# Paired half-height matmuls, two-chunk recurrence steps and early sums of squares in a fused two-block network

## The chip, the core and the metric

The kernel runs on one core of a Trainium2 chip. The metric is the device time of one execution in microseconds (us). Engines are named as the profile names them: PE (TensorE matmuls), PEld (its weight loads), DVE (VectorE), ACT (ScalarE), POOL (GpSimd) and SP (SyncE). Matmul results land in PSUM, which the kernel uses as eight banks, a0 to a3 and d0 to d3; a view of the profile shows them as `ps_a` and `ps_d`.

## What is computed

Two residual blocks over 512 tokens of width 1024, in float32, each with its own mixture of experts. Block 1 mixes a gated linear recurrence (HGRN2) with differential attention; block 2 mixes an RWKV-7 recurrence with a sparse attention, then a cross attention. What the change touches:

```python
# HGRN2, chunks of 64 tokens, 4 heads of 128
o = tril(q_rel k_rel^T) v + (q * exp(b)) S          # value products
S = exp(b_end) * S + k_end^T v                       # state update
o = rms_norm(o)
# differential attention, 4 heads, key width 64, four query blocks of 128
a = softmax(q1 k1^T / 8) - lam * softmax(q2 k2^T / 8)
o = rms_norm(a v)
# block 2, RWKV: two low-rank products (64 -> 512); sparse attention: 8 heads of width 64
w, a = tanh(xw) @ w2, xa @ a2
p = softmax(q_h k_h^T / 8 + mask);  o_h = p v_h      # causal, masked to selected keys
```

## The kernel before

The program is written as stages in Python order, and a scheduler fixes one static instruction order for each engine: it simulates a time line and takes the next instruction that is ready there. An engine then runs its list strictly in that order and waits at each entry for what that needs. Only instructions given to `keep_in_program_order` keep the written order among themselves.

Block 1's dense part is this. The normalised input (`hT`) is multiplied with the projection weights in `dense`, whose matmuls all carry the line of `mm` (L209): three passes over 128 x 512 tiles, `hT,wh`, `hT,wl` and a low part of `hT` with `wh`. Call these the dense matmuls. They need nothing of the attention, so the scheduler puts them between the steps of it. The attention (L542 to L569) takes 16 iterations, four heads with four query blocks of 128; iteration i has n = 128(i+1) keys. Each does two score matmuls with 64 rows (L550, banks a0 and a1), a causal mask added by a matmul (L551), a maximum on DVE (L552), exponentials on ACT (L555), the combination on DVE (L558 to L560), i+1 transposes (L564, bank a2) and a copy on ACT (L565); after a head come four value matmuls (L568). `aT` and `dv` are kept, and a norm over them (L572 to L588) makes `C`, the input of the first branch product.

The recurrence (L635 to L669) runs over 4 pairs of chunks in bank a3 alone: chunk scores (L643), a masking multiply (L645), transposes of the keys (L648), and for each chunk four state products with 64 rows (L658), four updates on DVE (L661) and, for each head, a 64-row value product (L666) and a 128-row state product (L667). `out_norm` then makes the input of the second branch product, which lies in `D`. Behind it stand the first branch products (`ps_d<-C,wh`) and the second (`ps_d<-D,wh`).

In block 2 the low-rank products (L1322, L1326) have 64 rows each, in the lower and the upper half; the sparse attention (L1671 to L1700) has the same shape as block 1's, with two heads e = 0, 1 for each of four p: scores L1679, mask L1682, maximum L1684, exponential L1687, scaling L1689, transposes L1692 and their copy L1693, value products L1698. Its scores take banks d0, d1 and a2 in turn, its transposes d2 and a3. Dense matmuls (`hT`, later the 96 with `r` and `k`) stand between its steps. After it comes the branch product `ps_d<-GG,wh`. The experts' stages, which stream weights, are not touched.

Of the kernel before, what the change touches and what calls it, by code (L numbers as in the profile page):

```python
# [177 lines left out]
class Net:  # L178
# [29 lines left out]
    def mm(self, *a, **k):  # L208
        self.pin(self.nc.tensor.matmul(*a, **k))  # L209

# [197 lines left out]
    def dense1(self, rings, late):  # L408
# [129 lines left out]

        for h in range(4):
            vh = dv[:, :, h * 128:(h + 1) * 128]  # L540
            aT = B.tile([128, 4, 512], F32, name="aT", bufs=2)
            for i in range(4):  # L542
# [19 lines left out]
                b = self.bank("a2")  # L562
# [3 lines left out]
            b = self.bank("a2")  # L566
# [6 lines left out]
        r = A.tile([128, 4, 8], F32, name="onr", bufs=2)  # L573
        b = self.bank("a", (128, 4, 8))
        for h in range(4):
            sq = k3([128, 512])
            nc.scalar.activation(sq.rearrange("p (j n) -> p j n", j=4), vv(h), AF.Square)
            self.tok_sums(b, sq, 2 * h, one2)
        nc.scalar.activation(r, b, AF.Sqrt, scale=1.0 / 128, bias=self.eps)
        nc.vector.reciprocal(r, r)  # L580
        for h in range(4):
            b = self.tok_spread(r, 2 * h, 1)
# [14 lines left out]
        self.banks("a3")  # L597
# [37 lines left out]
        S = B.tile([128, 4, 128], F32, name="hgS", bufs=2)  # L635
        nc.vector.memset(S, 0.0)
        for m in range(4):
            tok = slice(m * 128, (m + 1) * 128)
            b = self.bank("a", (128, 4, 64))
            for h in range(4):  # L640
                for p in range(2):
                    c = slice(m * 128 + p * 64, m * 128 + p * 64 + 64)
                    nc.tensor.matmul(b[p * 64:(p + 1) * 64, h, :], krel[:, h, c], qrel[:, h, c], start=True, stop=True)  # L643
            sc = k2([128, 4, 64])
            nc.vector.tensor_mul(sc, b, self.c("inc64")[:, None, :].broadcast_to([128, 4, 64]))  # L645
# [4 lines left out]
            nc.scalar.activation(ke, b, AF.Copy)  # L650
            for p in range(2):
                r = slice(p * 64, (p + 1) * 64)
                c = slice(m * 128 + p * 64, m * 128 + p * 64 + 64)
                So = S
                if 2 * m + p < 7:
                    bk = self.bank("a", (128, 4, 128))
                    for h in range(4):
                        nc.tensor.matmul(bk[:, h, :], ke[r, h, :], hv[r, m, h * 128:(h + 1) * 128], start=True, stop=True)  # L658
                    S = B.tile([128, 4, 128], F32, name="hgS", bufs=2)
                    for h in range(4):  # L660
# [1240 lines left out]
```

## Time and profile before

| | us |
|---|---|
| median of 3 runs (lowest to highest) | 2191.87 (2190.04 to 2196.93) |
| the profiled execution | 2193.93 |
| its span | 2192.2 |
| first attention score to first branch product, block 1 | 109.2 to 369.6 |
| first to second branch product, block 1 | 369.6 to 393.7 |
| end of RWKV's solve to sparse attention's branch product, block 2 | 1331.4 to 1467.5 |

The profile is of one execution; its time less its span, 1.7 us, lies outside the span. "Granted clock" is a share of TensorE's full 2.4 GHz; 0.50 is its lower level, 1.2 GHz. A float32 matmul of narrow tiles is shown as two records, and a record's printed length overlaps the next one's, so the time that one takes is read from start to start.

### The profile page before, as it was taken

The page shows a single profiled execution, that of the slowest core. Times are in us where ns is not written, and L with a number is a line of the kernel's source. Part 1 is how long each engine was busy: PE and PEld are TensorE (multiplying, and loading weights), DVE is VectorE, ACT ScalarE, POOL GpSimd, SP SyncE. Part 2 cuts the span into 40 slices and gives each one's busy share as a digit, 9 for nine tenths or more (in the row PEclk, how much of TensorE's full clock was granted, in tenths as well). Part 3 has the DMA queues.
Part 4 walks back from the last instruction along what each step waited for, and adds up shares of the span by engine and source line. Part 5 has one row for each costly group of instructions (what it writes and reads, how often), then busy time and mean ns, then how long its engine had stood idle before and what let it go on. Part 6 is the DMA issues. An engine that isn't in the chain of part 4 may idle for free. (4 is left out here: it accounts for less than half of the span.)

```text
span 2192.2 us, 29816 instructions
## 1 busy us (share of the span) xinstructions
PE 2116.7 (97%) x11946; PEld 1363.0 (62%) x11946; DVE 983.7 (45%) x2002; ACT 679.4 (31%) x1317; POOL 161.6 (7%) x138
## 2 busy tenths in 40 slices
PE   8999999999999999998989999999898999999996
PEld 6766778787544444445766775677778454444443
DVE  4674323563333332325388484445455232333334
ACT  5463333253111111114534333433443111111112
POOL 0420001200000000000252100001110000000000
PEclk9999899999999999998999999999999999999998
DMA  4211131377999999993222112112633899999994
GB/s 178 87 66 48 46 109 67 143 287 269 415 419 417 420 420 419 420 377 106 68 76 77 40 63 77 39 65 77 250 110 141 345 409 420 420 419 420 419 419 162
DMA packets 96318, 505.87 MB, mean 231 GB/s; under 512 B 21088, under 2 KB 26208, under 8 KB 44464
## 3 DMA queue, kind: packets, MB, share of 16 engines
q1 hardware_dynamic: 90992, 490.09, 56.3%
q10 hardware_dynamic: 4688, 11.66, 1.5%
q0 software_dynamic: 496, 2.17, 0.3%
q8 instruction: 96, 1.57, 0.3%
q14 instruction: 46, 0.38, 0.0%
HBM read 494.83 MB, written 8.91 MB: 230 GB/s over the span
## 5 line engine op out<-in xcount | busy, mean ns | idle before, releaser
L209 PE MATMUL ps_d<-wslot,xg 128*64 128x512 f32 x2048 | 446.4, 592 | 0.0
L209 PE MATMUL ps_d<-hT,wh 128*128 128x512 f32 x1056 | 348.0, 414 | 1.9 <-DVE hT L300 1.9
L209 PEld LDWEIGHTS ps_d<-wslot,xg 128*64 128x64 f32 x2048 | 148.3, 137 | 286.5 <-issue 276.5
L195 DVE TENSOR_TENSOR wl<-wslot,wh 128x512 fp32r<-128x512 f32 x236 | 168.6, 719 | 287.4 <-ACT wh L194 232.0
L194 ACT ACTIVATE wh<-wslot 128x512 fp32r<-128x512 f32 x260 | 163.2, 630 | 320.9 <-PE ps_d L209 255.8
L209 PEld LDWEIGHTS ps_d<-hT,wh 128*128 128x128 f32 x1056 | 199.7, 195 | 54.7 <-issue 9.3
L1010 DVE TENSOR_TENSOR s<-ps_d,s 128x512 f32<-128x512 f32 x32 | 22.1, 692 | 423.0 <-PE ps_d L209 423.0
L209 PE MATMUL ps_d<-hT,wl 128*128 128x512 f32 x528 | 210.3, 410 | 0.5 <-DVE wl L195 0.5
L209 PE MATMUL ps_a<-wslot,hidT 128*64 128x512 f32 (+1 forms) x832 | 178.3, 578 | 1.7 <-ACT hidT L1018 1.4
L209 PE MATMUL ps_d<-wh,hT 128*128 128x512 f32 x512 | 164.1, 397 | 3.0 <-DVE hT L300 1.4
L1048 DVE TENSOR_TENSOR acc<-acc,ps_a 128x512 f32<-128x512 f32 (+1 forms) x214 | 131.2, 664 | 54.9 <-PE ps_a L209 54.7
L209 PEld LDWEIGHTS ps_a<-wslot,hidT 128*64 128x64 f32 x832 | 58.7, 137 | 108.9 <-issue 100.4
L209 PE MATMUL ps_a<-yy,S 128*128 128x512 f32 (+1 forms) x428 | 114.6, 400 | 5.6 <-DVE acc L1048 5.6
L209 PEld LDWEIGHTS ps_d<-hT,wl 128*128 128x128 f32 x528 | 102.7, 195 | 25.4 <-issue 1.9
L209 PEld LDWEIGHTS ps_d<-wh,hT 128*128 128x128 f32 x512 | 95.7, 188 | 26.7 <-ACT wh L194 1.7
L985 ACT ACTIVATE xg<-ps_a,gain 128x256 f32<-128x256 f32 x102 | 48.2, 475 | 200.0 <-PE ps_a L209 200.0
L209 PE MATMUL ps_a<-oh,xs 128*128 128x256 f32 x816 | 107.1, 285 | 1.3 <-DVE oh L1137 1.3
L209 PEld LDWEIGHTS ps_a<-oh,xs 128*128 128x128 f32 x816 | 100.9, 191 | 9.6 <-issue 9.6
L1036 ACT ACTIVATE yy<-ps_a,gc 128x512 fp32r<-128x512 f32 (+1 forms) x52 | 34.9, 671 | 223.7 <-PE ps_a L209 192.2
L209 PE MATMUL ps_d<-wl,hT 128*128 128x512 f32 x256 | 101.8, 397 | 1.8 <-DVE wl L195 1.8
L209 PEld LDWEIGHTS ps_a<-yy,S 128*128 128x128 f32 x428 | 74.8, 188 | 31.4 <-DVE acc L1048 13.6
L1009 ACT ACTIVATE s<-ps_d 128x512 f32<-128x512 f32 x32 | 19.1, 598 | 199.3 <-PE ps_d L209 199.3
(584 smaller groups left out, 2838.2 us busy)
## 6 DMA issues: line engine op xcount, KB each, us to landing
wslot<-in_wm_dram SPq DMA_DIRECT2D x380, 1024.0 KB, 11.6
wslot<-in_wd_dram SPq DMA_DIRECT2D x108, 512.0 KB, 3.6
wslot<-in_wd_dram SPq DMA_DIRECT2D x19, 1024.0 KB, 14.7
wslot<-in_wm_dram SPq DMA_DIRECT2D x8, 512.0 KB, 15.0
C<-in_x_dram SPq DMA_DIRECT2D x4, 512.0 KB, 5.2
acc<-in_x_dram ACTq DMA_DIRECT2D x4, 512.0 KB, 4.8
kvd<-kvs ACTq DMA_DIRECT2D x8, 256.0 KB, 4.1
xd<-acc ACTq DMA_DIRECT2D x1, 2048.0 KB, 11.9
```

Of the source, the lines that this page charges most:

```text
L194: self.nc.scalar.activation(hi, src, AF.Copy)
L195: (lo_eng or self.nc.vector).tensor_sub(lo, src, hi.bitcast(F32))
L209: self.pin(self.nc.tensor.matmul(*a, **k))
L985: nc.scalar.activation(xg[:, k, :n], b[:, :n], AF.Copy, scale=gain[:, k:k + 1])
L1009: nc.scalar.activation(s1, hb[0], AF.Silu)
L1010: nc.vector.tensor_mul(s1, hb[1], s1)
L1036: nc.scalar.activation(y[0][:, c], b, AF.Copy, scale=gcol)
L1048: nc.vector.tensor_add(acc[:, t, c], acc[:, t, c], b)
```

## The change

`side_by_side` issues two matmuls that use opposite row halves one after the other, upper half first, and keeps all such pairs in program order. It is used for the scores of both attentions, for the state products of two chunks, and for the low-rank products. In the attentions the transposes go into the bank of the scores; block 1's attention and recurrence now share all four a banks; the sparse attention takes (d0, d1) and (d2, a2) by turns. The recurrence treats two chunks as one step: the masked scores sit in a 128 x 128 block-diagonal tile (zeroed once on POOL), so that one full-height value product serves both chunks, and the state products add to the same bank. Squares and their sums are taken as each head or each pair of chunks ends.

```diff
+    def side_by_side(self, xs, stop=True):
+
+
+        for o, l, r in xs[::-1]:
+            self.tc.keep_in_program_order(self.nc.tensor.matmul(o, l, r, start=True, stop=stop))
...
+        def scales(r):
+
+            nc.scalar.activation(r, r, AF.Sqrt, scale=1.0 / 128, bias=self.eps)
+            nc.vector.reciprocal(r, r)
...
-                ps = []
-                for m in range(2):
-                    r = slice(m * 64, (m + 1) * 64)
-                    b = self.bank("a%d" % m)
-                    nc.tensor.matmul(b[:, :n], qkT[r, 0, h, qs], qkT[r, 1, h, :n], start=True, stop=False)
+                ps, sb = [], [self.bank("a") for _ in range(2)]
+                self.side_by_side([(sb[m][:, :n], qkT[m * 64:m * 64 + 64, 0, h, qs], qkT[m * 64:m * 64 + 64, 1, h, :n])
+                                   for m in range(2)], stop=False)
+                for m, b in enumerate(sb):
                     nc.tensor.matmul(b[:, qs], idb, dgn, start=False, stop=True)
                     nc.vector.reduce_max(st[:, m:m + 1], b[:, :n], axis=AX.X)
                     nc.vector.tensor_scalar(st[:, 2 + m:3 + m], st[:, m:m + 1], -0.125, None, op0=ALU.mult)
...
-                b = self.bank("a2")
+                b = sb[0]
...
-            b = self.bank("a2")
+            b = self.bank("a")
...
-        self.banks("a0", "a1", "a2")
+            sq = k4([128, 512])
+            nc.scalar.activation(sq, b, AF.Square)
+            b = self.bank("a", (128, 4, 2))
+            self.tok_sums(b, sq, 0, one2)
+            nc.vector.tensor_copy(rd[:, :, 2 * h:2 * h + 2], b)
...
+        scales(rd)
...
+        S = B.tile([128, 4, 128], F32, name="hgS", bufs=3)
...
+        scs = [k3([128, 4, 128]) for _ in range(2)]
+        for t in scs:
+            nc.gpsimd.memset(t, 0.0)
...
-            sc = k2([128, 4, 64])
-            nc.vector.tensor_mul(sc, b, self.c("inc64")[:, None, :].broadcast_to([128, 4, 64]))
+                    nc.tensor.matmul(b[rs[p], h, :], krel[:, h, cs[p]], qrel[:, h, cs[p]], start=True, stop=True)
+            sc = scs[m % 2]
+            for p in range(2):
+                nc.vector.tensor_mul(sc[rs[p], :, rs[p]], b[rs[p]],
+                                     self.c("inc64")[rs[p], None, :].broadcast_to([64, 4, 64]))
...
+
+            Ss = [S]
+            bks = [self.bank("a", (128, 4, 128)) for _ in range(2 if m < 3 else 1)]
+            for h in range(4):
+                hc = slice(h * 128, (h + 1) * 128)
+                self.side_by_side([(bk[:, h, :], ke[rs[p], h, :], hv[rs[p], m, hc]) for p, bk in enumerate(bks)])
+            for p, bk in enumerate(bks):
+                S = B.tile([128, 4, 128], F32, name="hgS", bufs=3)
+                for h in range(4):
+                    nc.vector.scalar_tensor_tensor(S[:, h, :], Ss[p][:, h, :], eend[:, h, 2 * m + p:2 * m + p + 1],
+                                                   bk[:, h, :], op0=ALU.mult, op1=ALU.add)
+                Ss.append(S)
+            bo = self.bank("a", (128, 4, 128))
+            for h in range(4):
+                nc.tensor.matmul(bo[:, h, :], hv[:, m, h * 128:(h + 1) * 128], sc[:, h, :], start=(h == 0), stop=False,
+                                 skip_group_check=True)
...
-                    for h in range(4):
-                        nc.tensor.matmul(bk[:, h, :], ke[r, h, :], hv[r, m, h * 128:(h + 1) * 128], start=True, stop=True)
-                    S = B.tile([128, 4, 128], F32, name="hgS", bufs=2)
-                    for h in range(4):
-                        nc.vector.scalar_tensor_tensor(S[:, h, :], So[:, h, :], eend[:, h, 2 * m + p:2 * m + p + 1],
-                                                       bk[:, h, :], op0=ALU.mult, op1=ALU.add)
-                bo = self.bank("a", (128, 4, 64))
                 for h in range(4):
-                    vh = hv[r, m, h * 128:(h + 1) * 128]
-                    nc.tensor.matmul(bo[:, h, :], vh, sc[r, h, :], start=True, stop=False)
-                    nc.tensor.matmul(bo[:, h, :], So[:, h, :], qe[:, h, c], start=False, stop=True)
-                nc.scalar.activation(oT[:, :, c], bo, AF.Copy)
+                    nc.tensor.matmul(bo[:, h, rs[p]], Ss[p][:, h, :], qe[:, h, cs[p]], start=False, stop=(p == 1 and h == 3),
+                                     skip_group_check=True)
+            nc.scalar.activation(oT[:, :, tok], bo, AF.Copy)
...
+            sq = k2([128, 4, 128])
+            nc.scalar.activation(sq, bo, AF.Square)
+            b = self.bank("a", (128, 8))
+            for h in range(4):
+                nc.tensor.matmul(b[:, 2 * h:2 * h + 2], sq[:, h, :], one2, start=True, stop=True)
+            nc.vector.tensor_copy(rh[:, m, :], b)
...
+        scales(rh)
...
-            b = self.bank("a")
-            nc.tensor.matmul(b, lora[0:64, pc], xw[0:64], start=True, stop=True)
+            wb = [self.bank("a") for _ in range(2)]
+            self.side_by_side([(wb[e], lora[e * 64:e * 64 + 64, pc], xw[e * 64:e * 64 + 64]) for e in range(2)])
...
+            bo_ = self.bank(("d3", "a3")[p % 2])
...
-                sb = []
-                for e in range(2):
-                    r = slice(e * 64, e * 64 + 64)
-                    b = self.bank(("d0", "d1", "a2")[(turn + e) % 3])
-                    nc.tensor.matmul(b[:, :n], qT[r, p, qs], KT[r, p, :n], start=True, stop=False)
-                    sb.append(b)
+                sb = [self.bank((("d0", "d1"), ("d2", "a2"))[turn % 2][e]) for e in range(2)]
+                turn += 1
+                self.side_by_side([(sb[e][:, :n], qT[e * 64:e * 64 + 64, p, qs], KT[e * 64:e * 64 + 64, p, :n])
+                                   for e in range(2)], stop=False)
...
-                    b = self.bank(("d2", "a3")[turn % 2])
```

The changed kernel's lines are some 6 to 11 higher than those of before; its pairs all carry L215. Two places show how the order moves on PE.

The first is in block 1. Before, on PE in the middle of the recurrence, attention scores and masks (L550, L551), dense matmuls (L209) and state products of a chunk (L658) stand among one another.

```order
L550 MATMUL ps_a_1091<-C 128x128
L551 LDWEIGHTS idb
L551 MATMUL ps_a_1091<-dgn,idb 128x128
L209 MATMUL ps_d_2030<-hT_92,wh 128x512
L209 MATMUL ps_d_2030<-hT_91,wl 128x512
L209 MATMUL ps_d_2031<-hT_91,wh 128x512
L658 MATMUL ps_a_1792<-F,k_1770 128x128
L550 MATMUL ps_a_1105<-C 128x256
L551 LDWEIGHTS idb
L551 MATMUL ps_a_1105<-dgn,idb 128x128
L658 MATMUL ps_a_1792<-F,k_1770 128x128 x3
```

Small and dense rows alternate here in groups of one to six.

After, at the end of block 1's attention (L215 on `C` scores, L561 mask, L574 transposes, L578 value products): the last dense matmul stands ahead of head 3's third set of transposes.

```order
L209 MATMUL ps_d_2591<-hT_92,wh 128x512
L209 MATMUL ps_d_2591<-hT_91,wl 128x512
L574 MATMUL ps_a_1138<-cst,k_1145 128x128 x3
L215 MATMUL ps_a_1161<-C 128x512
L215 MATMUL ps_a_1160<-C 128x512
L561 LDWEIGHTS idb
L561 MATMUL ps_a_1160<-dgn,idb 128x128
L561 LDWEIGHTS idb
L561 MATMUL ps_a_1161<-dgn,idb 128x128
L574 MATMUL ps_a_1160<-cst,k_1167 128x128 x4
L578 MATMUL ps_a_1182<-aT,dv 128x512
L578 MATMUL ps_a_1182<-aT,dv 128x384
```

Behind its first two rows no dense matmul follows until the first branch product: the scores of the last block stand behind the transposes of the one before.

Further on in the same list, the last two steps of the recurrence (L215 on `F` state products, L682 products with the state, L654 chunk scores, L661 key transposes, L689 sums, L678 value products) and the first branch product (`C,wh`):

```order
L215 MATMUL ps_a_1889<-F,k_1886 128x128
L215 MATMUL ps_a_1888<-F,k_1886 128x128
L682 MATMUL ps_a_1908<-E,hgS 128x64 x4
L654 MATMUL ps_a_1930<-acc 64x64 x8
L661 MATMUL ps_a_1941<-cst,D 128x128 x4
L689 MATMUL ps_a_1924<-one_680,k_1922 128x2 x4
L678 MATMUL ps_a_1958<-k_1747,F 128x128 x4
L215 MATMUL ps_a_1948<-F,k_1946 128x128 x4
L682 MATMUL ps_a_1958<-E,hgS 128x64 x8
L689 MATMUL ps_a_1974<-one_680,k_1972 128x2 x4
L209 MATMUL ps_d_2754<-C,wh 128x512 x2
L209 MATMUL ps_d_2754<-C,wl 128x512
```

So what stood among dense matmuls now stands behind them: 674 dense rows lie between the first score and the first branch product in both lists, in the changed one all of them ahead of the last two iterations' transposes and of the whole recurrence, in blocks of about 36 to 42 between two iterations.

Second place, the sparse attention on PE, before: one block's value products (L1698), another's transposes (L1692) and two others' scores (L1679) follow one another, with dense matmuls behind.

```order
L1698 MATMUL ps_d_10552<-GG_10275,X_8929 64x128 x7
L1692 MATMUL ps_a_10714<-cst,k_10710 128x128
L1679 MATMUL ps_a_10753<-VU,qT 128x384
L1692 MATMUL ps_d_10731<-cst,k_10727 128x128 x2
L1682 LDWEIGHTS X_7481
L1682 MATMUL ps_a_10753<-X_7481 128x384
L1679 MATMUL ps_d_10787<-VU,qT 128x512
L1682 LDWEIGHTS X_7481
L1682 MATMUL ps_d_10787<-X_7481 128x512
L209 MATMUL ps_a_11117<-r,wh 128x512
L209 MATMUL ps_a_11117<-k,wh 128x512
L209 MATMUL ps_a_11117<-r,wl 128x512
```

After, the same attention at p = 1 (L1698 transposes, L1703 value products, L215 scores, L1689 masks; `ps_a_10476` and `ps_d_10475` are the banks of the 512-key block):

```order
L1698 MATMUL ps_d_10441<-cst,k_10449 128x128 x3
L1698 MATMUL ps_d_10442<-cst,k_10461 128x128 x3
L1703 MATMUL ps_a_10384<-GG_10253,X_8907 64x128 x6
L215 MATMUL ps_a_10476<-VU,qT 128x512
L215 MATMUL ps_d_10475<-VU,qT 128x512
L1689 LDWEIGHTS X_7459
L1689 MATMUL ps_d_10475<-X_7459 128x512
L1689 LDWEIGHTS X_7459
L1689 MATMUL ps_a_10476<-X_7459 128x512
L1698 MATMUL ps_d_10475<-cst,k_10483 128x128 x4
L1698 MATMUL ps_a_10476<-cst,k_10496 128x128 x4
L1703 MATMUL ps_a_10384<-GG_10253,X_8907 64x128 x8
```

Each block's transposes and value products stand ahead of the next block's scores. Between the end of the solve and the branch product there are 288 dense rows in both lists; in the changed one they are all used ahead of p = 1's second transposes, in blocks of 24, and the ten iterations after that (p = 1, i = 2 and 3; p = 2; p = 3) have none.

## Rows read from the trace of the kernel before

**Rows 1.** The line of the page on the engines (busy us, share of the span, instructions) and, of its 40 slices of the span, that of the clock granted to TensorE (tenths of full speed).

```profile
PE 2116.7 (97%) x11946; PEld 1363.0 (62%) x11946; DVE 983.7 (45%) x2002; ACT 679.4 (31%) x1317; POOL 161.6 (7%) x138
...
PEclk9999899999999999998999999999999999999998
```

**Rows 2.** Busy time of each engine in three stretches: from the first diff-attention score to the first branch stage, that branch stage, and from the end of block 2's state solve to its branch stage. Columns: stretch, its length, busy us (instructions) of PE, weight loads, DVE, ACT, POOL; then the granted clock, the DMA share and GB/s.

```profile
109.20:369.60 260.40, 259.92 (x1203) 192.84 (x1202) 111.51 (x239) 109.04 (x223) 11.22 (x8) 0.95 0.19 66
369.60:393.70 24.10, 23.74 (x106) 18.76 (x105) 16.17 (x24) 8.41 (x15) 5.82 (x4) 1.00 0.26 86
1331.40:1467.50 136.10, 136.10 (x646) 87.23 (x647) 63.17 (x175) 57.25 (x142) 0.00 (x0) 1.00 0.17 59
```

**Rows 3.** What TensorE waited for in the first of those stretches (us in total, times, longest); for the third stretch the same view has no row.

```profile
PE ps_d L209 <- DVE wl L195: 0.5, 1, 0.5
```

**Rows 4.** TensorE in order of time, block 1's attention and recurrence (start us, modelled length, engine, line, tiles, partitions*columns, records): one unpaired score instruction among dense matmuls, dense matmuls at two clocks, and one chunk's value products.

```profile
192.08 1.12 PE L550 MATMUL ps_a<-C 64*128 64x512 f32 x2
193.13 0.23 PE L551 MATMUL ps_a<-dgn,idb 128*128 128x128 bf16 x1
...
256.00 1.05 PE L209 MATMUL ps_d<-hT,wh 128*128 128x512 f32 x2
...
258.56 0.95 PE L209 MATMUL ps_d<-hT,wh 128*128 128x512 f32 x2
259.35 0.40 PE L209 MATMUL ps_d<-hT,wl 128*128 128x512 f32 x1
...
260.97 0.39 PE L209 MATMUL ps_d<-hT,wh 128*128 128x512 f32 x1
...
270.00 0.40 PE L209 MATMUL ps_d<-hT,wl 128*128 128x512 f32 x1
270.33 0.43 PE L666 MATMUL ps_a<-k,F 64*128 64x64 f32 x2
270.69 0.43 PE L667 MATMUL ps_a<-E,hgS 128*128 128x64 f32 x2
...
273.32 1.20 PE L209 MATMUL ps_d<-hT,wh 128*128 128x512 f32 x2
```

**Rows 5.** The same view for two sets of four block-2 matmuls whose operands lie by turns in the two row halves.

```profile
1183.90 1.19 PE L209 MATMUL ps_a<-pT 64*128 64x256 f32 x4
1185.01 0.73 PE L209 MATMUL ps_d<-hT,wh 128*128 128x512 f32 x2
...
1186.61 0.70 PE L209 MATMUL ps_a<-pT 64*128 64x256 f32 x4
1187.24 0.50 PE L209 MATMUL ps_d<-hT,wh 128*128 128x512 f32 x1
```

**Rows 6.** All engines in order of time, block 2's attention: value products and transposes on PE, then the softmax of one 256-key block (a mask matmul, the maximum, its scaling, the exponential and its sum).

```profile
1427.28 0.87 PE L1698 MATMUL ps_d<-GG,X 128*64 128x128 f32 x10
...
1428.08 0.66 PE L1692 MATMUL ps_a<-cst,k 128*128 128x128 f32 x4
...
1429.92 0.28 PE L1682 MATMUL ps_d<-X 128*128 128x256 bf16 x1
...
1430.24 0.42 DVE L1684 TENSOR_REDUCE st<-ps_d 128x1 f32<-128x256 f32 x1 [2.66 <-PE ps_d L1682]
...
1430.94 0.48 ACT L1687 ACTIVATE k<-ps_d,st 128x256 f32<-128x256 f32 x1 [0.95 <-DVE st L1685]
...
1431.32 0.19 ACT L1687 ACTIVATION_READ_ACCUMULATOR k<-ps_d,st 128x1 f32 x1
```

**Rows 7.** Groups of instructions by line and shape in the third stretch, those of 512 keys: busy us, mean ns of one, idle time before them.

```profile
L1684 DVE TENSOR_REDUCE st<-ps_d 128x1 f32<-128x512 f32 x6 | 4.2, 692 | 2.2 <-PE ps_d L1682 2.1
L1689 DVE TENSOR_SCALAR k<-k,st 128x512 f32<-128x512 f32 x8 | 3.9, 485 | 0.3
...
L1687 ACT ACTIVATE k<-ps_d,st 128x512 f32<-128x512 f32 x6 | 4.1, 682 | 0.6 <-DVE st L1685 0.6
...
L1693 ACT ACTIVATE GG<-ps_d 128x512 f32<-128x512 f32 x4 | 2.4, 597 | 2.1 <-PE ps_d L1692 2.0
```

**Rows 8.** The same in the first stretch: the state update, attention's last combination, the copy of the transposed keys, and a load of an activation table.

```profile
L661 DVE SCALAR_TENSOR_TENSOR hgS<-hgS,eend,ps_a 128x128 f32<-128x128 f32 x28 | 7.9, 342 | 6.9 <-PE ps_a L658 6.8
...
L560 DVE SCALAR_TENSOR_TENSOR k<-k,da_st,k 128x512 f32<-128x512 f32 x4 | 3.0, 748 | 0.1
...
L650 ACT ACTIVATE k<-ps_a 128x512 f32<-128x512 f32 x4 | 2.4, 589 | 1.4 <-PE ps_a L648 1.4
...
L579 ACT ACT_TABLE_LOAD x1 | 1.3, 1283 | 0.0
```

**Rows 9.** Stretches of 3.4 us around the places where the granted clock falls (columns as in rows 2).

```profile
1112.40:1115.80 3.40, 1.28 (x20) 0.70 (x18) 3.30 (x4) 2.01 (x4) 1.79 (x2) 1.00 0.14 43
1115.80:1119.20 3.40, 3.00 (x82) 2.79 (x83) 3.40 (x5) 0.00 (x0) 2.32 (x2) 0.53 0.33 116
...
1166.80:1170.20 3.40, 1.48 (x64) 1.21 (x64) 3.30 (x8) 0.00 (x0) 0.00 (x0) 1.00 0.35 136
1170.20:1173.60 3.40, 2.30 (x64) 1.98 (x64) 3.19 (x11) 0.00 (x0) 0.00 (x0) 0.56 0.00 0
1173.60:1177.00 3.40, 2.85 (x11) 2.59 (x12) 3.19 (x10) 1.20 (x2) 0.88 (x1) 0.50 0.00 0
...
201.20:204.60 3.40, 3.40 (x11) 2.72 (x10) 0.47 (x1) 1.44 (x5) 0.00 (x0) 0.50 0.00 0
```

More of the change, by code (lines that the diff above doesn't have):

```diff
@@ L569, in dense1 @@
             nc.scalar.activation(vh, b.rearrange("p (j n) -> p j n", j=4), AF.Copy)
-        self.banks("a0", "a1", "a2")
+            sq = k4([128, 512])
[3 more added lines that the diff above has]
+            nc.vector.tensor_copy(rd[:, :, 2 * h:2 * h + 2], b)
         yd = big("C", (128, 2, 4, 512), F32R)
         vv = lambda h: dv[:, :, h * 128:(h + 1) * 128]
-        r = A.tile([128, 4, 8], F32, name="onr", bufs=2)
-        b = self.bank("a", (128, 4, 8))
+        scales(rd)
         for h in range(4):
[L576 to L580, printed above, removed]
-        for h in range(4):
-            b = self.tok_spread(r, 2 * h, 1)
+            b = self.tok_spread(rd, 2 * h, 1)
             o = k3([128, 512])
@@ L594, in dense1 @@
         dense(8, hT, "N", lambda j, b: nc.scalar.activation(hv[:, j, :], b, AF.Copy))
-        self.banks("a3")
         bb = big("G")
@@ L634, in dense1 @@
         oT = big("G")
-        S = B.tile([128, 4, 128], F32, name="hgS", bufs=2)
+        S = B.tile([128, 4, 128], F32, name="hgS", bufs=3)
         nc.vector.memset(S, 0.0)
+        rh = A.tile([128, 4, 8], F32, name="onr", bufs=2)
+        scs = [k3([128, 4, 128]) for _ in range(2)]
+        for t in scs:
+            nc.gpsimd.memset(t, 0.0)
         for m in range(4):
             tok = slice(m * 128, (m + 1) * 128)
+            cs = [slice(m * 128 + p * 64, m * 128 + p * 64 + 64) for p in range(2)]
+            rs = [slice(p * 64, p * 64 + 64) for p in range(2)]
             b = self.bank("a", (128, 4, 64))
@@ L641, in dense1 @@
                 for p in range(2):
-                    c = slice(m * 128 + p * 64, m * 128 + p * 64 + 64)
-                    nc.tensor.matmul(b[p * 64:(p + 1) * 64, h, :], krel[:, h, c], qrel[:, h, c], start=True, stop=True)
-            sc = k2([128, 4, 64])
-            nc.vector.tensor_mul(sc, b, self.c("inc64")[:, None, :].broadcast_to([128, 4, 64]))
+                    nc.tensor.matmul(b[rs[p], h, :], krel[:, h, cs[p]], qrel[:, h, cs[p]], start=True, stop=True)
[3 more added lines that the diff above has]
+                                     self.c("inc64")[rs[p], None, :].broadcast_to([64, 4, 64]))
             b = self.bank("a", (128, 4, 128))
@@ L669, in dense1 @@
-        self.d("o_hgT", oT)
-        def out_norm(o, gcol, out):
-            r = A.tile([128, 4, 8], F32, name="onr", bufs=2)
-            b = self.bank("a", (128, 4, 8))
-            for h in range(4):
-                sq = k2([128, 512])
-                nc.scalar.activation(sq, o(h), AF.Square)
-                self.tok_sums(b, sq, 2 * h, one2)
-            nc.scalar.activation(r, b, AF.Sqrt, scale=1.0 / 128, bias=self.eps)
-            nc.vector.reciprocal(r, r)
-            for h in range(4):
-                b = self.tok_spread(r, 2 * h, 1)
-                nc.vector.scalar_tensor_tensor(out(h), o(h), gcol, b, op0=ALU.mult, op1=ALU.mult)
@@ new lines, in dense1 @@
+            nc.scalar.activation(oT[:, :, tok], bo, AF.Copy)
[5 more added lines that the diff above has]
+            nc.vector.tensor_copy(rh[:, m, :], b)
+        self.d("o_hgT", oT)
+        scales(rh)
+        for h in range(4):
+            b = self.tok_spread(rh, 2 * h, 1)
+            nc.vector.scalar_tensor_tensor(oT[:, h, :], oT[:, h, :], gh[:, 0:1], b, op0=ALU.mult, op1=ALU.mult)
@@ L1320, in dense2 @@
             pc = slice(p * 128, (p + 1) * 128)
-            b = self.bank("a")
-            nc.tensor.matmul(b, lora[0:64, pc], xw[0:64], start=True, stop=True)
+            wb = [self.bank("a") for _ in range(2)]
+            self.side_by_side([(wb[e], lora[e * 64:e * 64 + 64, pc], xw[e * 64:e * 64 + 64]) for e in range(2)])
             ld = tmp[:, p, 0]
-            nc.scalar.activation(ld, b, AF.Tanh, scale=0.5, bias=hw0[:, p:p + 1])
-            b = self.bank("a")
-            nc.tensor.matmul(b, lora[64:128, pc], xw[64:128], start=True, stop=True)
+            nc.scalar.activation(ld, wb[0], AF.Tanh, scale=0.5, bias=hw0[:, p:p + 1])
             th = tmp[:, p, 1]
-            nc.scalar.activation(th, b, AF.Tanh, scale=0.5, bias=ha0[:, p:p + 1])
+            nc.scalar.activation(th, wb[1], AF.Tanh, scale=0.5, bias=ha0[:, p:p + 1])
             nc.gpsimd.tensor_scalar(ld, ld, hc, hc, op0=ALU.mult, op1=ALU.add)
```

11 lines of the change are left out of this document (1 added, 10 removed).

## The prediction

> **What bounds the kernel now.** I read the page's line on the engines first: PE is busy for 2,116.7 of 2,192.2 us at a clock close to full [rows 1]. So the span is PE's list of work, and what matters is where PE would come to wait. The stretches that the change touches say more. In block 1, from the first attention score to the first branch product, PE is busy for 259.92 of 260.40 us, at a mean clock of 0.95; the branch product behind it takes 24.10 us; in block 2, from the solve to the sparse attention's branch product, PE is busy for all 136.10 us [rows 2]. The view of waits agrees: 0.5 us in block 1's stretch, none in block 2's [rows 3]. In both the attention's softmax runs on DVE and ACT while PE does dense matmuls, so that it costs only PE's own matmuls. Two questions follow: how much PE work goes, and whether there is still dense work to stand over the softmax.
>
> **Prices.** A full-clock dense record takes 0.231 us (seven from 259.35 to 260.97), a half-clock one 0.427 (six from 256.00 to 258.56) [rows 4]. A change from dense to small matmuls costs about 0.10 more (270.33 less 270.00, against 0.231). An unpaired 512-key score instruction takes 1.05 us (192.08 to 193.13) [rows 4], about 0.26 for every 128 keys. A 128-column record of transposes or value products takes 0.08 to 0.10 (ten from 1427.28 to 1428.08) [rows 6].
>
> **Do pairs run side by side?** Four matmuls in alternate row halves take 1.11 us in one place and 0.63 in another [rows 5]. I take the second as the pair's price, so a pair costs what one instruction did, and the first as its bound: no gain.
>
> **Block 1, the part with cover.** The changed list has 674 dense records, 155.7 us at full clock; the 16 score pairs, 4 x (0.26 + 0.53 + 0.79 + 1.05) = 10.5; some 150 short records (masks, transposes, three heads' value products and sums) at 0.10, 15; and 42 changes between dense and small work, 4.2. Together 185.4 us. From 109.2 on, the dense work is used up at about 295, with no dense matmul left for what follows. Before, the same work had 120 such changes, unpaired scores, and the recurrence among it; a stretch at half clock is in rows 9 (201.20).
>
> **Block 1, the part without cover.** First the end of the attention. For 512 keys at full clock: pair and mask 1.5 us, two maxima 1.4 and their scaling 0.3 on DVE, two exponentials with their sums 1.75 on ACT, two combinations 1.4, transposes and their copy 1.2 [rows 6 to 8]; this 7.5 and some 4 that are left of the 384-key block, then value products 2.2, square and sums 2.4, a table load 1.28 with root and reciprocal 0.7, and the spreading matmuls 3.4: 22 us, 26 if PE is at half clock. Then the recurrence. A step's chain runs over the copy and square of the step before (0.59 each and a hop: 1.4), its sums 0.8, value products 0.8, half of the state products 0.4, the paired products 0.8, a hop 0.3, four updates 4 x 0.342 = 1.4 and the other half 0.4 [rows 8]: 6.3 us at full clock, 9.5 at half, 25 to 38 for four. So the last step ends 47 to 64 us after 295; I take 59, mostly half clock, because a list of short matmuls with waits is what stands ahead of the half-clock stretches in rows 9.
>
> The first branch product needs only the attention's norm, so it starts right after the last sums (2 us) and runs 24.1 [rows 2]. But the og stage's multiplication now waits for the recurrence's norm, which ends later than the branch product's banks need it: 4 us more on PE, which waited 0.3 there before. One or two further us at half clock at its start make 32. The second branch product would start at 295 + 59 + 32 = 386 instead of 393.7: **8 us gained**, 22 at full clock throughout, 3 lost at half.
>
> **Block 2, the low-rank products.** Four pairs save at most 4 x 1.05 = 4.2 us; but what follows is bound by DVE (busy 3.30 of 3.40 us at 1112.40 [rows 9]), which gets its first inputs in another order. **2 us gained**, between 4 gained and 2 lost.
>
> **Block 2, the sparse attention.** A block's PE work for n keys before was 1.65, 2.7, 3.7 and 4.8 us (scores at 0.26 per 128 keys and head record pair, mask 0.1, transposes and value products at 0.08 to 0.15). The ten blocks that have no dense work now held 34 us of the 136.10; pairing the other six saves 4; 24 fewer changes save 2 to 3. That leaves 95; a sum from below (288 dense records 66.5, changes 3, and the rest of the list) gives 88. I take 92 to the last dense matmul. Then ten blocks in which nothing covers the softmax: the next pair stands behind the transposes and value products of the block before. The chain at 512 keys and full clock: pair 1.05, mask to maximum 0.4, two maxima 1.38, scaling and hop 0.25, two exponentials with their sums 2 x 0.78, reciprocal and scaling 0.75, last transposes 0.55, copy with hops 0.8, value products 1.3: 8.0 us. With 384, 256 and 128 keys it is 6.8, 5.4 and 4.1 [rows 6, 7]. Two rounds of all four and one of the two longest make 63. At half clock PE's share doubles, to 10.8, 8.9, 7.0 and 5.1, in all 83.
>
> Which clock? In the trace it falls after PE was busy for 1.28 of 3.40 us, and after 1.48 of 3.40; and once low it stayed low through a stretch with 2.30 busy [rows 9]. The 512-key chain has PE busy for 3.0 of 8.0 us at full clock, and 6 of 10.8 at half; the 128-key one for less. So I take 78, near the half-clock end. The Trainium skill says the same in a general form ("TensorE: Matmul & The Clock Gate", section "Loop structure matters more than you think"): matmuls that follow back to back keep the engine warm, a wait ahead of every one lets it go cold. By that page alone the sum would be the one with half clock throughout, 2,237. The branch product's own start at half clock costs 1. So 92 + 78 + 1 = 171 instead of 136.1: **35 us lost**, 20 at full clock, 40 at half.
>
> **Costed at nothing.** The two POOL memsets, the second masking multiply on DVE, the third state buffer and the early squares lie far from their readers, or beside DVE and ACT that are idle for more than half of the stretch [rows 2]. Bank changes alone do nothing to PE's list beyond what the order shows. Their cover is the dense work, up to 295; without it the squares are in the chain above. The experts' stages start later or earlier by the shift; they stream at a rate that does not depend on it.
>
> **Sum.** 2,193.9 (profiled execution) - 8 - 2 + 35 = 2,219; the median of before is 2 lower, so 2,217.
>
> **Rivals.**
> *Full clock in the uncovered parts.* If the engine stays at 2.4 GHz, the sum is -22 - 4 + 20 = -6: 2,186. For it: blocks with 3 us of PE work among waits are nowhere in the trace, and at 1112.40 the clock is still 1.00 in the stretch with the gap itself. Against: the stretches behind such gaps.
> *A shorter chain in the sparse attention.* If one head's maximum, exponential and scaling run beside the other's fully, a block costs about 2 us less (the second maximum and exponential hidden): at full clock a mean of 4.4 us and not 6.3, ten blocks 44. Then 92 + 44 = 136, no loss there, and block 1 decides: -22 - 4 + 0, 2,166. With block 1 at -8 the kernel is no slower once a mean block takes 5.3 us (92 + 1 + 53 against 136 + 10), and faster beyond 0.3% below 4.7; I have 7.8. Against: DVE's list has both maxima ahead of both scalings, so that ACT starts late, and PE's has both heads' transposes ahead of the value products.
> *PE's work decides.* If waits stayed covered, all saved PE time would count: half the scores of both attentions (12 + 12), low-rank 4, value products 17 (2.99 for each of eight chunks [rows 4] against 6 to 7 in all at 0.10 and 0.05 a record), state products 3, and 10 of block 1's half-clock loss (a mean clock of 0.95 over 260 us [rows 2]): 2,134. Against: the order after has no dense rows there, whatever the waits.
> *Pairs do not overlap* (second half waits, as at 1183.90 in rows 5): 10.5 + 11.8 + 4 and some state products come back: 2,217 + 25 = 2,242.
>
> **How the numbers follow.** My forecast (uncovered parts mostly at half clock, pairs side by side) has 0.62, and 2,204 to 2,234 as its own range; full clock 0.14; the shorter chain 0.08; PE's work 0.06; no overlap 0.10. The range takes in the forecast, no more than its upper bound (3 and 2 lost, 40 lost: 2,237), and full clock: 2,186 to 2,237. A measurement of this kernel tells 0.3%, 6.6 us, from no change. Faster by more: the shorter chain, PE's work, and the faster part of full clock, 0.17; within it 0.11 (the rest of full clock and the forecast's low tail); slower 0.72.
>
> **What would show it.** In block 1: dense matmuls end near 295, PE idle in most of the 60 us behind, the second branch product near 386. In block 2: PE busy up to about 92 us after the solve, then ten blocks of 4 to 11 us with PE waiting on DVE and ACT, clock 0.50 in most of them; pairs whose two instructions start within 0.05 us. The prediction is wrong if the clock stays at 1.00 there, if a mean uncovered block takes below 6 us, or if the recurrence's steps take below 6 each.

## The result and the profile after

The changed kernel takes 2,209.6 us (median; 2,206.6 to 2,211.1) where the kernel before took 2,191.0 in the same runs: 1.008 times as long, 95% interval 1.0056 to 1.0104, so 0.8% slower. The prediction was 2,217, between 2,186 and 2,237, slower with 0.72. The profiled execution took 2,210.3 us, its span is 2,208.4.

The lines of the page that answer to [rows 1]:

```profile
PE 2083.7 (94%) x11910; PEld 1356.9 (61%) x11914; DVE 991.4 (45%) x2014; ACT 678.2 (31%) x1313; POOL 162.6 (7%) x140
...
PEclk9999988999999999998999999869999999999998
```

PE is busy for 33 us less than before, and the span is 16 longer: work went, and waits came. The stretches of [rows 2], cut where the last dense matmul stands (columns as there): block 1 up to the last dense matmul, to the end of attention and norm, the recurrence, and the first branch product; block 2's attention up to its last dense work, its ten uncovered blocks, and both together:

```profile
109.20:293.40 184.20, 183.96 (x855) 143.03 (x853) 91.19 (x187) 87.44 (x183) 12.55 (x8) 1.00 0.24 83
293.40:316.20 22.80, 12.49 (x45) 7.95 (x45) 7.25 (x16) 7.54 (x17) 0.00 (x0) 0.63 0.00 0
316.20:342.40 26.20, 24.30 (x257) 21.94 (x256) 14.74 (x45) 6.91 (x13) 1.05 (x2) 1.00 0.20 71
346.30:380.50 34.20, 29.28 (x112) 22.85 (x113) 16.84 (x26) 11.04 (x17) 5.85 (x4) 0.85 0.16 52
1317.90:1408.10 90.20, 89.67 (x425) 65.79 (x426) 41.28 (x93) 33.80 (x75) 0.00 (x0) 1.00 0.26 91
1408.10:1481.20 73.10, 48.45 (x220) 26.81 (x222) 21.99 (x80) 22.13 (x62) 0.00 (x0) 0.66 0.01 4
1317.90:1482.40 164.50, 138.15 (x642) 92.60 (x646) 63.28 (x173) 57.05 (x140) 0.00 (x0) 0.85 0.15 52
```

The second branch product now starts at 380.5 instead of 393.7, 13.2 us earlier. The sparse attention takes 164.5 us instead of 136.1, 28.4 more. Between the two the distance is 0.3 us shorter (937.4 against 937.7), behind them 1.3 longer: together the 16.2 us of the two spans. PE is busy in the last stretch for 138 us, about as long as before; but that is partly half clock, and 26 us of waits stand beside it. The view of waits shows on what (PE's line and what it waits for, us in total, times, longest):

```profile
PE ps_d L1698 <- DVE st L1695: 23.4, 10, 2.9
...
PE ps_a L574 <- DVE k L570: 7.6, 2, 4.5
...
PE ps_d L209 <- DVE k L712: 5.3, 2, 4.6
```

The first two have no row before [rows 3]; the third lies in the first branch product, where PE waited 0.4 us in all before. Ten waits of the transposes (L1698) for the scaled probabilities are the ten uncovered blocks. One such block of 512 keys in order of time:

```profile
1444.23 1.22 PE L215 MATMUL ps_a<-VU,qT 64*128 64x512 f32 x1
...
1444.24 1.22 PE L215 MATMUL ps_d<-VU,qT 64*128 64x512 f32 x1
...
1446.35 0.69 DVE L1691 TENSOR_REDUCE st<-ps_d 128x1 f32<-128x512 f32 x1 [5.26 <-remote]
1446.96 0.68 DVE L1691 TENSOR_REDUCE st<-ps_a 128x1 f32<-128x512 f32 x1
...
1447.79 0.69 ACT L1694 ACTIVATE k<-ps_d,st 128x512 f32<-128x512 f32 x1 [5.08 <-DVE st L1692]
...
1448.47 0.68 ACT L1694 ACTIVATE k<-ps_a,st 128x512 f32<-128x512 f32 x1
...
1449.44 1.09 PE L1698 MATMUL ps_d<-cst,k 128*128 128x128 f32 x4 [2.91 <-DVE st L1695]
...
1451.31 2.72 PE L1703 MATMUL ps_d<-GG,X 128*64 128x128 f32 x16
...
1453.96 0.80 PE L215 MATMUL ps_d<-VU,qT 64*128 64x128 f32 x4
```

The two halves of the scores start 0.01 us apart, so pairs do run side by side. Then DVE takes both maxima and ACT both exponentials, PE waits 2.91 us, transposes and value products follow, and only behind them the next pair (1453.96): 9.7 us for a block, at a mean clock of 0.68. Four of the ten blocks are at 0.50 from end to end, the others between 0.68 and 0.88.

### The profile page after: what moved, and what is told of

Its sections match the earlier page's. It is cut to its first block, busy times and chain, and to the rows that moved or that the text cites. A ratio compares the mean times of both kernels' runs of the same rounds, so it can differ in the third digit from the quotient of the medians.

```text
span 2208.4 us, 29777 instructions
## 1 busy us (share of the span) xinstructions
PE 2083.7 (94%) x11910; PEld 1356.9 (61%) x11914; DVE 991.4 (45%) x2014; ACT 678.2 (31%) x1313; POOL 162.6 (7%) x140
## 5 line engine op out<-in xcount | busy, mean ns | idle before, releaser
L209 PE MATMUL ps_d<-wslot,xg 128*64 128x512 f32 x2048 | 446.4, 592 | 0.0
L209 PE MATMUL ps_d<-hT,wh 128*128 128x512 f32 x1056 | 333.5, 403 | 2.2 <-DVE hT L306 2.2
L209 PEld LDWEIGHTS ps_d<-wslot,xg 128*64 128x64 f32 x2048 | 148.3, 137 | 286.5 <-issue 274.5
L209 PEld LDWEIGHTS ps_d<-hT,wh 128*128 128x128 f32 x1056 | 194.6, 190 | 50.5 <-issue 6.6
L209 PE MATMUL ps_d<-hT,wl 128*128 128x512 f32 x528 | 201.2, 396 | 0.0
L209 PE MATMUL ps_a<-wslot,hidT 128*64 128x512 f32 (+1 forms) x832 | 178.2, 578 | 1.7 <-ACT hidT L1029 1.4
L209 PE MATMUL ps_d<-wh,hT 128*128 128x512 f32 x512 | 163.9, 397 | 2.7 <-ACT wh L194 1.5
L209 PEld LDWEIGHTS ps_a<-wslot,hidT 128*64 128x64 f32 x832 | 58.7, 137 | 108.9 <-issue 100.4
L209 PE MATMUL ps_a<-yy,S 128*128 128x512 f32 (+1 forms) x428 | 114.6, 400 | 5.6 <-DVE acc L1059 5.6
L209 PEld LDWEIGHTS ps_d<-hT,wl 128*128 128x128 f32 x528 | 99.9, 189 | 22.9 <-issue 0.6
L209 PEld LDWEIGHTS ps_d<-wh,hT 128*128 128x128 f32 x512 | 95.8, 188 | 26.9 <-ACT wh L194 2.4
L209 PE MATMUL ps_a<-oh,xs 128*128 128x256 f32 x816 | 107.1, 285 | 1.5 <-DVE oh L1148 1.5
L209 PEld LDWEIGHTS ps_a<-oh,xs 128*128 128x128 f32 x816 | 100.9, 191 | 9.8 <-issue 9.7
L209 PE MATMUL ps_d<-wl,hT 128*128 128x512 f32 x256 | 101.3, 396 | 1.8 <-DVE wl L195 1.8
L209 PEld LDWEIGHTS ps_a<-yy,S 128*128 128x128 f32 x428 | 74.8, 188 | 31.4 <-DVE acc L1059 13.6
```

## The experiments

Each was timed in rounds with the kernel before on the same chip; times are given as a difference from that. "Second branch product" is the start of the product from `D` in block 1 (393.7 before, 380.5 in the changed kernel), "sparse stretch" the time from the last spreading matmul behind the solve to the branch product from `GG` (136.1 and 164.5).

**1. The sparse attention as before.** The loop of before in place of the changed one (`side_by_side` and the two bank pairs out, `self.bank(("d0", "d1", "a2")[(turn + e) % 3])` and the plain matmuls in).

> The changed kernel with the sparse attention of before (unpaired scores, no pins, banks d0, d1, a2 in turn, transposes in d2 and a3); the rest of the change stays. Theory (each stage's change of time is its own): the sparse attention's 28.7 us go, block 1's 13 stay: 2,209.6 - 29 = 2,181, between 2,176 and 2,185; second branch product of block 1 near 380, sparse stretch near 136. Rival (block 1's gain is given back later, in the experts' stages whose weights start to stream earlier): 2,188 to 2,192, no faster than before.

Measured: 2,183.3 against 2,196.0, ratio 0.9949 (0.9932 to 0.9965), 12.7 us faster. The second branch product starts at 379.5, the sparse stretch is 136.0. The stage alone turns the sign of the change, and block 1's gain of 13 to 14 us arrives at the end, within the interval.

**2. Only the second instruction of a pair pinned.**

```diff
-        for o, l, r in xs[::-1]:
-            self.tc.keep_in_program_order(self.nc.tensor.matmul(o, l, r, start=True, stop=stop))
+        for k, (o, l, r) in enumerate(xs[::-1]):
+            i = self.nc.tensor.matmul(o, l, r, start=True, stop=stop)
+            if k:
+                self.tc.keep_in_program_order(i)
```

> The changed kernel with one line of the helper changed: only the second instruction of a pair is pinned, behind its first; the first may stand ahead of the transposes and value products of the block before. Theory (the pin of the first, not the pairing nor the banks, empties the cover): the sparse stretch falls from 165 to 122 to 130 us with no long waits on the scaling, block 1's attention is covered again and its second branch product starts between 360 and 370; in all 2,145 to 2,165. Rival (two bank pairs that also take the transposes let no block run ahead): sparse stretch above 150, in all 2,195 to 2,210.

Measured: 2,170.3 against 2,196.0, ratio 0.9898 (0.9880 to 0.9917), 25.7 us faster. Of the sparse stretch (columns as in rows 2):

```profile
1313.00:1437.00 124.00, 120.27 (x642) 82.27 (x645) 62.08 (x173) 55.46 (x140) 0.00 (x0) 1.00 0.19 69
```

124.0 us at full clock, with hardly a wait: 12.1 us less than before, which is half of its scores. So pairs and banks are sound, and the pin of the first instruction alone costs this stage 40.5 us (164.5 against 124.0). `keep_in_program_order` puts an instruction behind the one that was written before it on its engine, which here is the last value product of the block before. Block 1's second branch product starts at 373.6, later than the theory's 360 to 370, and the total lies above the range given. The trace of this run shows two reasons. The first is in the attention (PE, block 1):

```profile
263.91 1.12 PE L215 MATMUL ps_a<-C 64*128 64x512 f32 x2
264.97 0.23 PE L563 MATMUL ps_a<-dgn,idb 128*128 128x128 bf16 x1
...
270.56 1.12 PE L215 MATMUL ps_a<-C 64*128 64x512 f32 x2
271.62 0.23 PE L563 MATMUL ps_a<-dgn,idb 128*128 128x128 bf16 x1
```

The two scores of one 512-key block stand 6.65 us apart with dense matmuls between, each at the unpaired price (1.06 us from its start to the mask behind it). Eleven of block 1's sixteen pairs stand apart like this, and such a pair gains nothing; experiment 5 tests why. The second reason is the recurrence: the attention has its dense matmuls again, but they end at 314.7, and from 315.6 to the first branch product at 340.1 the recurrence stands without any.

**3. The recurrence in banks of its own.** Experiment 2, with `self.banks("a0", "a1")` ahead of block 1's attention, `self.banks("a2", "a3")` ahead of the recurrence, and the masked scores in a buffer of their own.

> As the run with the second pinned, and the recurrence has two banks of its own (a2, a3; the attention a0, a1) and its masked scores a buffer of their own, so that it stands among dense matmuls again; the last head's last three blocks and the norm stay uncovered. Theory (the shared banks and buffers put the recurrence behind the attention): some 24 us of uncovered recurrence go, some 15 of uncovered attention come: second branch product between 355 and 372, in all 2,140 to 2,162. Rival (the recurrence's steps cost the same wherever they stand, because PE's own work in them is the limit): like the run with the second pinned within 4 us.

Measured: 2,179.9 against 2,196.0, ratio 0.9942 (0.9923 to 0.9960): 16.1 us faster, 9.6 us slower than experiment 2, so theory and rival both missed. The second branch product starts at 386.1. The recurrence does stand among dense matmuls; but in the attention's two banks its pairs stand apart, and its last blocks are behind the dense matmuls, one by one:

```profile
326.50:362.30 35.80, 22.23 (x65) 11.57 (x63) 17.71 (x36) 13.93 (x30) 5.43 (x4) 0.64 0.04 15
```

35.8 us with PE busy for 22 at a clock of 0.64. My estimate of that end (15 us lost) was too low. The run changes banks and buffer together, so it does not tell which of them lets the recurrence go ahead of the attention's end. What leaves the recurrence bare in the changed kernel was still open here; experiments 7 and 9 say more.

**4. PE kept busy in the uncovered blocks.** In nine of the ten:

```diff
+                nxt = [self.bank((("d0", "d1"), ("d2", "a2"))[turn % 2][e]) for e in range(2)] if turn < 16 else None
+                if nxt and 4 * p + i >= 6:
+                    for _ in range((7, 9, 10, 12)[i]):
+                        self.tc.keep_in_program_order(nc.tensor.matmul(nxt[0], idb, bias[:, 0:512], start=True, stop=True))
```

> The changed kernel; in nine of the sparse attention's ten uncovered blocks 7 to 12 idle 512-column matmuls (bf16, about 0.22 us each, into the next block's bank, overwritten by its scores) stand between the masks and the transposes, where PE waits. Theory (part of the loss is the half clock of PE's own matmuls in these blocks): the clock stays at 1.00, the ten blocks take 62 to 66 us instead of 73, in all 2,197 to 2,203. Rival (the chain over DVE and ACT sets the blocks' length at either clock): 72 to 76 us, in all 2,208 to 2,213.

Measured: 2,201.3 against 2,196.0, ratio 1.0029 (1.0017 to 1.0041): 5.3 us slower than before, 13.4 better than the 18.7 of the changed kernel. The ten blocks:

```profile
1409.60:1470.20 60.60, 53.28 (x304) 26.46 (x308) 22.02 (x80) 22.14 (x62) 0.00 (x0) 0.98 0.01 5
```

60.6 us at a clock of 0.98, instead of 73.1 at 0.66: work that nobody uses makes the stage 12.5 us faster. From the first maximum to the first transposes a 512-key block takes 3.09 us in both (1446.35 to 1449.44 in the block above, 1440.27 to 1443.36 here), so DVE and ACT do the same at the same pace; what got shorter are PE's own matmuls. The chain at full clock is even a little below the 63 us that the prediction worked out. Of the 40.5 us that the pin costs, about 12.5 are the clock; 28 are left at a clock of 0.99 (a stretch of 151.9 us in this run against 124.0), which is the softmax without cover.

**5. Block 1's pairs lower half first.** Experiment 2, and `for m in (1, 0)` in the list that block 1's attention hands to the helper (which reverses it): the lower half's bank comes free later, because the transposes use it.

> As the run with the second pinned, but block 1's score pairs are issued lower half first. In that run's order most of these pairs stand apart, because the instruction that comes first gets its bank earlier than the second; here it gets it later, and 12 of 16 pairs stand together in the order. Theory (pairs gain only where they stand next to each other, half of their cost): some 8 us less in block 1's dense part than with the second pinned (second branch product near 366), 26 to 36 us below the kernel before in all. Rival (pairs gain nothing where dense work covers the softmax anyway): as with the second pinned within 3 us.

Measured: 2,161.0 against 2,194.6, ratio 0.9848 (0.9823 to 0.9873), 33.6 us faster. The second branch product starts at 369.2, 4.4 us earlier than in experiment 2, against 8 expected and at most 3 by the rival. Most pairs now stand together, with both scores of 512 keys in 1.06 us:

```profile
264.88 1.13 PE L215 MATMUL ps_a<-C 64*128 64x512 f32 x4
265.94 0.28 PE L563 MATMUL ps_a<-dgn,idb 128*128 128x128 bf16 x2
```

Up to 335.6, where the first branch product starts, the clock's mean is 0.98, and 1.00 in the stretch up to it in experiment 2: dense work ends sooner, and part of the recurrence behind it falls to half clock.

**6. Block 1's attention alone.** The kernel before with this attention, pinned, banks a0 to a2; recurrence in a3 and sparse attention as before.

> The kernel before with block 1's attention of the change (pinned pairs, early sums; banks a0 to a2) and the low-rank pairs; recurrence (in a3) and sparse attention as before. Theory: the recurrence stands among dense matmuls, the attention's last two blocks and its norm behind the last of them; pairs give 10.5 us, the uncovered end takes 12 to 18: second branch product between 392 and 400, in all 0 to 7 us above the kernel before. Rival (block 1's 13 us come from the pairs): 8 to 13 us below it.

Measured: 2,197.1 against 2,194.6, ratio 1.0011 (1.0000 to 1.0023), 2.5 us slower. The second branch product starts at 401.0, 7.3 us later than before and 1 beyond the range given. What lies behind the last dense matmul, up to the first branch product:

```profile
342.00:378.20 36.20, 17.54 (x70) 10.38 (x67) 17.25 (x37) 12.35 (x28) 5.25 (x4) 0.62 0.01 3
```

36.2 us, 17.5 of them busy, at a clock of 0.62. Its pairs stand together and save half of the scores' price, and more is lost at the end. That only 2.5 of the 7.3 us are left in the total cannot be put down to a stage: from the second branch product to the end of the solve the traces of these runs take between 934.1 and 943.2 us, though none of them changes anything there but the low-rank pairs, which all nine have.

**7. The recurrence alone.** The kernel before with the recurrence of the change in four a banks, both attentions as before.

> The kernel before with the recurrence of the change (two chunks a step, full-height value products, pinned state pairs, four a banks) and the low-rank pairs; both attentions as before. In its order the attention keeps its cover, and dense matmuls stand between all steps of the recurrence. Theory (the value products' alternation cost 17 us of PE's time and most of the half-clock stretches, and in the change the pinned attention uses up the cover of the recurrence): second branch product between 362 and 372, in all 20 to 32 us below the kernel before. Rival (the recurrence's steps are slow by their chain over ACT and DVE, wherever they stand): near 380 and 13 us below, as in the changed kernel.

Measured: 2,170.2 against 2,194.6, ratio 0.9897 (0.9874 to 0.9921), 24.4 us faster. Second branch product at 368.1, 25.6 us earlier. The end of the stretch and the first branch product:

```profile
300.00:343.10 43.10, 42.76 (x238) 36.05 (x236) 15.94 (x35) 16.73 (x27) 0.00 (x0) 1.00 0.33 115
...
343.10:368.10 25.00, 23.38 (x97) 17.77 (x97) 14.88 (x21) 8.59 (x15) 6.38 (x4) 1.00 0.25 84
```

PE is busy for 42.8 of the 43.1 us ahead of the first branch product, at full clock, and dense matmuls stand between the recurrence's steps, which use the same four banks as in the changed kernel. So the shared banks alone do not leave it bare. In both kernels it stands behind the spreading matmuls of the attention's norm; these start at 257.2 here and at 313.0 in the changed kernel, whose attention takes up to 42 dense matmuls between two of its blocks. So it is the changed attention that uses up the recurrence's cover. The pin of the first instruction is only a part of that: without it, in experiment 2, the spreading still starts at 299.0. In experiment 9, which has pairs but the banks and the late sums of before, it starts at 266.0; whether banks or sums hold the attention back in experiment 2, no run takes apart. Alone the two parts of block 1 give +7.3 and -25.6, in sum -18.3; together -13.2.

**8. The recurrence, and the sparse attention with its second pinned.** Experiment 7 with the changed sparse loop and experiment 2's helper.

> The recurrence of the change, block 1's attention as before, the sparse attention and the low-rank products of the change, only the second of each pair pinned. Theory (stages add up): 20 to 32 us from block 1 and 12 from the sparse attention: 32 to 44 us below the kernel before. Rival (the gain of one stage is given back in the experts' stages): below 28.

Measured: 2,157.4 against 2,194.6, ratio 0.9832 (0.9807 to 0.9856), 37.2 us faster: experiment 7's 24.4 and the sparse attention's 12.1 add up. The sparse stretch is 124.0 us.

**9. Everything covered.** Experiment 8, and

```diff
-                    b = self.bank("a%d" % m)
-                    nc.tensor.matmul(b[:, :n], qkT[r, 0, h, qs], qkT[r, 1, h, :n], start=True, stop=False)
+                ps, sb = [], [self.bank("a%d" % m) for m in range(2)]
+                self.side_by_side([(sb[m][:, :n], qkT[m * 64:m * 64 + 64, 0, h, qs], qkT[m * 64:m * 64 + 64, 1, h, :n])
+                                   for m in range(2)], stop=False)
```

> As the combined run, and block 1's attention has its score pairs too (second pinned behind the first), in banks a0 and a1 with the transposes in a2 as before, so that the scores' banks come free after the exponentials. In its order the pairs stand together and dense matmuls stand behind nearly every step of attention and recurrence. Theory (pairs pay half of the scores' 21 us once nothing is uncovered): second branch product between 354 and 360, 8 to 11 us below the combined run, 43 to 52 below the kernel before. Rival (the recurrence's last two steps and the norm lose what the pairs give): within 4 us of the combined run.

Measured: 2,154.6 against 2,194.7, ratio 0.9822 (0.9804 to 0.9839), 40.1 us faster, the fastest here; 2.9 us ahead of experiment 8, which the intervals do not tell apart. This is below the 43 to 52 us of the theory. The first branch product starts at 326.3, 14.8 us earlier than in experiment 8, the second at 360.9, only 4.9 earlier:

```profile
109.20:326.30 217.10, 215.81 (x1166) 169.30 (x1164) 112.61 (x245) 104.94 (x218) 13.99 (x10) 1.00 0.23 81
326.30:360.90 34.60, 29.18 (x113) 22.73 (x113) 16.96 (x26) 10.91 (x17) 5.84 (x4) 0.85 0.15 49
```

The branch product between them takes 34.6 us where it takes 24.5 in experiment 8: PE waits 5.2 us in it for the output gate's product (L716), ahead of which ACT waits 8.2 us for the multiplication with the normed recurrence (L717), and PE runs at a clock of 0.85. So the theory holds up to 326.3, and the rival for the whole: ten of the fifteen us are given back right behind, by the stage that reads the recurrence's result.

## Why the prediction was right

The sign and its cause hold. Block 1 gained, the sparse attention lost more, because blocks whose scores stand behind the transposes and value products of the block before have nothing to run beside their softmax; experiments 1 and 2 show it by taking the stage, and then the one pin, away. Step by step:

*Dense work ends near 295* in block 1: 293 (292.81 starts the last one). *Attention's end 22 to 26 us*: 22.8, at a clock of 0.63.

*Recurrence 25 to 38 us, mostly at half clock*: 26.2, at a clock of 1.00. Here the step that failed is the clock; the full-clock sum of 6.3 us a step was close (a mean of 6.55). I counted PE's own work in a step at 3.2 us, and it is 6.4. A record of the products with the state was taken at 0.05 us, for which there was no row, and it takes 0.12 (eight in 0.93, 325.27 to 326.20). And the next step's chunk scores and key transposes (L654 and L661, 1.24 us from 328.96 to 330.20) were left out, though the order has them where PE was to wait:

```profile
324.30 1.14 PE L678 MATMUL ps_a<-k,F 128*128 128x128 f32 x8
325.27 1.00 PE L682 MATMUL ps_a<-E,hgS 128*128 128x64 f32 x8
326.20 1.16 PE L215 MATMUL ps_a<-F,k 64*128 64x128 f32 x16
327.81 1.21 PE L682 MATMUL ps_a<-E,hgS 128*128 128x64 f32 x8 [0.45 <-DVE hgS L673]
328.96 0.69 PE L654 MATMUL ps_a<-acc 128*64 128x64 f32 x16
329.62 0.66 PE L661 MATMUL ps_a<-cst,D 128*128 128x128 f32 x4
330.20 1.05 PE L689 MATMUL ps_a<-one,k 128*128 128x2 f32 x8
331.12 1.14 PE L678 MATMUL ps_a<-k,F 128*128 128x128 f32 x8
...
334.63 1.21 PE L682 MATMUL ps_a<-E,hgS 128*128 128x64 f32 x8 [0.45 <-DVE hgS L673]
```

A step takes 6.8 us (327.81 to 334.63) and has one wait of half a microsecond; PE is busy for 24.3 of 26.2 us. This is not a list of waits, though it has no dense matmul in it. The page of the Trainium skill that the prediction named, "TensorE: Matmul & The Clock Gate", section "Loop structure matters more than you think", counts as good a loop whose matmuls stay back to back, and as bad one with a long DMA wait ahead of every matmul, in which the engine goes cold. The trace agrees for this stretch: its matmuls follow each other with little wait, and the clock stays at 1.00. It does not always hold: in experiment 5 the same steps run at 1.00 twice (6.8 us each), and the clock falls within the last, after waits of 0.45 and 0.74 us (321.63 and 325.81).

*From the recurrence's end to the second branch product, 32 us*: 38.1 (342.4 to 380.5). 3.9 go until the first branch product starts, and the wait on the og stage was 4.6, as said; but after it the clock is low again, and the branch product takes 34.2 us at 0.85. Together block 1 gave 13.2 instead of 8 us: 12 too many up to the recurrence's end (354 against 342.4), 6 too few behind it. One bound of this part does not follow from its terms: with half clock throughout, 295 + 64 + 32 is 391, which is 3 us gained and not 3 lost.

*Low-rank products 2 us*: not shown either way. The distance between the two stages is 0.3 us shorter, but over the traces of the nine experiments, which all have these pairs, it lies between 934.1 and 943.2, so 2 us cannot be read from it.

*Sparse attention 92 + 78 + 1*: 90.2, 73.1 and 1.2. The ten blocks lie between the two bounds (63 and 83), since the clock's mean was 0.66; experiment 4 measures the full-clock end. The loss was 28.4 instead of 35.

Two of the prediction's own signs failed with the clock: PE was to be idle in most of the time behind block 1's last dense matmul, and was so for 14 of 53 us; and the clock was to be at 0.50 in most of the ten blocks, and was so in four.

The full-clock rival fell by the two stretches at 0.63 and 0.66, though it had the recurrence right, the shorter chain by a mean block of 7.3 us (it decided below 5.3), the one of pairs that do not overlap by 1444.23 and 1444.24. The one where PE's work decides fell by the order, as the prediction said; experiment 9, where nearly all is covered, brings 40 us of the 58 that it counted.

## What to carry to other kernels

A pin behind "what was written before" orders more than the pair that it is meant for: pin the second of two instructions to the first and leave the first free, and look in the order for what now stands between a matmul and the wait that it used to cover. Count the filler: work that hides a chain can be spent once, and a stage that takes more of it leaves a later one bare, so that the gain of one part depends on the other. Of two instructions that are to stand together, issue first the one whose buffer comes free last.

## What the runs showed of the hardware

Matmuls of no use in the waits made a stage 12.5 us faster by the clock (60.6 against 73.1 us, at 0.98 against 0.66), with DVE and ACT at the same pace. In the recurrence, records of 128 columns (L678), of 64 (L682) and of 2 (L689), each with weights of its own, take 0.12, 0.12 and 0.12 us in the lines above (eight in 0.97, 0.93 and 0.92), so the moving columns do not set their price. Nor does the number of instructions: the chunk scores (L654), of 64 columns too but with weights of 64 columns instead of 128, take 0.04 (sixteen in 0.66). The loads of the 128-column weights take as long as the records themselves, 0.97 us for eight of each kind; that they set the price fits these rows, but no run tests it.

Two instructions on opposite row halves paid the price of one only where they stood next to each other: 1.06 us for both scores of 512 keys in experiment 5, 1.06 for each in experiment 2.
